# Keeping the attention's output in DRAM as its two float32r parts in a two-layer encoder trunk

## The chip, the cores and the metric

The kernel runs on one core of a Trainium2 chip. The metric is the device time of one execution in microseconds (us). TensorE (PE) multiplies, VectorE (DVE), ScalarE (ACT) and GpSimd (POOL) work on elements, and SyncE (SP) issues all of the DMAs that this text speaks of. SP takes its instructions one after the other, so a DMA that has to wait holds up all that stand behind it.

## The reference, cut to what matters

Two layers over 1024 tokens of 1024 features, in float32. Layer 0 mixes tokens by a neighbourhood attention (NA, 16 heads of 64), layer 1 by a differential attention (DA, 8 heads of 128). Both end in an output projection of the heads' results, which a normalised residual follows:

```python
def neighborhood_attention(h, w_qkv, rpb, w_o):
...
    o = lax.map(row_fn, jnp.arange(rows))
    o = o.transpose(1, 0, 3, 2, 4).reshape(B, S, D)
    return o @ w_o

def diff_attention(h, w_qkv, lam, subln_g, w_o, t5_table, lambda_init):
...
    o = o.transpose(1, 2, 0, 3, 4).reshape(B, DA_HEADS, S, 2 * DA_HEAD_DIM)
    o = rms_norm(o, subln_g) * (1.0 - lambda_init)
    o = o.transpose(0, 2, 1, 3).reshape(B, S, D)
    return o @ w_o
...
        x = x + rms_norm(m, g[1])
        f = conv_glu_ffn(rms_norm(x, g[2]), ffn_w_in[i], ffn_conv_w[i], ffn_conv_b[i], ffn_w_out[i])
```

After that comes a gated feed-forward part of width 2816, and a gate on a per-layer input embedding.

## The kernel before

**The arithmetic.** A float32 matrix is split into two float32r parts: hi, which ACT makes by a copy that rounds, and lo = value - hi, which DVE makes by a subtraction (`split`, L81 to L91; with a scale, lines 88 and 89). A product is then three matmuls: hi by hi, hi by lo, lo by hi.

**The attention's output `oT`** is a scratch tensor in DRAM with the shape (8, 128, 1024): eight head pages (a pair of NA heads, or one DA head) of 128 features by 1024 tokens.
- In NA (`na_values`) the two heads of a pair are added into the page `opage` (tag "oT", one buffer) half by half: ACT copies one half of a PSUM bank to `low` (L434), DVE adds (L435). After the last of a pair's eight chunks L439 stores the page, 512 KB. In the chunk's other work ACT makes the softmax's exponentials (L368), and copies half of the next values' projection to SBUF (L307), which PE then transposes (L135); PE transposes the softmax pages at L410, and ACT and DVE split what comes out. A pair is j, 0 to 7.
- In DA (`da_values`, `da_out`) each of a head's eight chunks of 128 queries ends with its values times the softmax weights (L553), an RMS norm (L556, L557, L119, L559), a transpose on PE (L567), a scaled copy on ACT from PSUM into `ot` (L575, 128x128) and a store of 64 KB (L576). Two `ot` buffers take turns.
- The last page (j or h = 7) is not stored: it stays in SBUF in a buffer of the pool `raw`.

**The output projection.** `out_part(layer, t)` loads the first seven pages of 128 tokens, 448 KB in rows of 512 bytes, into a buffer of `raw` (L646), and splits it into two buffers of `ws`: one ACT instruction and one DVE instruction of 128x896. `raw` has 3 buffers and `ws` has 4, for all of the kernel's loads and split operands. The projection weights `W` come through `raw` too, eight loads of 512 KB (L96) that are split into resident pages.
- `first_out` runs beside the last attention head. It loads and splits W, and does token tile 0 for the first seven pages. `embeddings` runs beside it: it makes eight pages `e` in `ws`, and stores each in `pp` (L1119).
- `mix_out` takes the token tiles in the order 0, 4, 1, 5, 2, 3, 6, 7. For each it multiplies (48 matmuls, L637), normalises and adds the residual. The part of the tile two places later is made ready behind it (`load`, L679 to L683): `out_part`, the split of the last page's 128 columns, and the load of the residual's rows. Two parts fill the four `ws` buffers.

**What sets the order.** PE's order is written out by hand. The other engines' order is set by a scheduler when the kernel is built, from the program's order and what each instruction needs; an instruction stands in its engine's queue and holds up what stands behind it.

Of the kernel before, what the change touches and what calls it, by code (L numbers as in the profile page):

```python
# [8 lines left out]
F32 = mybir.dt.float32  # L9
F32R = mybir.dt.float32r  # L10
AF = mybir.ActivationFunctionType
# [4 lines left out]
P = 128  # L16
D = 1024
SEQ = 1024
NT = SEQ // P
KT = D // P  # L20
# [18 lines left out]
class Trunk:  # L39
# [374 lines left out]
    def na_values(self, x, n, oT):  # L414
        nc = self.nc
        j, m, g = n // 8, n // 4 % 2, n % 4
        V = self.v[2 * j]
        _, _, blocks, hi, lo = self.chunk.pop(n)
        if g % 2 == 0:
            self.o = self.av.tile([P, 512], F32, tag="av", name=self.uid("av"))  # L420
        o = self.o
        steps = [(2 * g, 0, 2, 0), (2 * g + 1, 0, 2, 2)] + [(kb, u, 1, 4 + i) for i, (kb, u) in enumerate(blocks[4:])]
        for i, (kb, u, w, at) in enumerate(steps):
            out = o[:, (2 * g % 4 + u) * P : (2 * g % 4 + u + w) * P]
            for z, a in enumerate((hi, lo)):
                nc.tensor.matmul(  # L426
                    out, V[:, kb, m], a[:, at * P : (at + w) * P], start=i + z == 0, stop=i == len(steps) - 1 and z == 1
                )
        if n % 8 == 0:
            self.opage = self.page(self.raw, "raw") if j == KT - 1 else self.page(x, "oT", bufs=1)  # L430
        if g % 2:
            h = g // 2 * 512
            low = self.page(x, "low", (P, 512), bufs=1)
            nc.scalar.activation(low[0:64], o[64:128], AF.Copy)  # L434
            nc.vector.tensor_tensor(  # L435
                out=self.opage[64 * m : 64 * m + 64, h : h + 512], in0=o[0:64], in1=low[0:64], op=ALU.add
            )
        if n % 8 == 7 and j < KT - 1:
            nc.sync.dma_start(oT[j], self.opage)  # L439

    def na(self, hT, oT, first, mid):

# [119 lines left out]
    def da_out(self, x, n, oT):  # L562
        nc = self.nc
        h, t = n // NT, n % NT
        b, os = self.chunk.pop(n)
        tr = b[:, P : 2 * P]
        nc.tensor.transpose(tr, os, self.ident)  # L567
        cols = slice(t * P, t * P + P)
        if h == D_HEADS - 1:
            if t == 0:  # L570
                self.opage = self.page(self.raw, "raw")
            nc.scalar.activation(self.opage[:, cols], tr, AF.Copy, scale=self.subg)
        else:
            ot = self.page(x, "ot", (P, P))
            nc.scalar.activation(ot, tr, AF.Copy, scale=self.subg)  # L575
            nc.sync.dma_start(oT[h][:, cols], ot)  # L576

    def da(self, hT, oT, first, mid):

# [62 lines left out]

    def out_part(self, layer, t):

        raw = self.page(self.raw, "raw", (P, KT - 1, P))
        self.nc.sync.dma_start(raw, self.oT[layer][: KT - 1, :, t * P : t * P + P].rearrange("j p t -> p j t"))  # L646
        hi, lo = self.page(self.ws, "ws", (P, KT, P), F32R), self.page(self.ws, "ws", (P, KT, P), F32R)
        self.split(raw, hi[:, : KT - 1], lo[:, : KT - 1])
        return hi, lo

    def first_out(self, layer):

# [498 lines left out]

    def run(self):
        i = self.i
        self.oT = [self.scratch(f"oT{n}", (KT, P, SEQ)) for n in range(2)]
        x1 = [self.scratch(f"x1_{n}", (SEQ, D)) for n in range(2)]
        self.pp = [self.scratch(f"pp{n}", (SEQ, D)) for n in range(2)]
        x3 = [self.scratch("x3", (SEQ, D)), self.out]
# [86 lines left out]
```

## Time and profile before

| | us |
|---|---|
| median of 3 runs (lowest to highest) | 2787.24 (2779.03 to 2789.44) |
| the profiled execution, its own time | 2781.16 |
| its span from the first to the last instruction | 2779.2 |
| PE busy | 2703.0 (97%) |
| DVE busy | 1985.5 (71%) |
| ACT busy | 1344.3 (48%) |
| DMA, 298.48 MB | 107 GB/s over the span |

The difference of 2.0 us between the profiled execution's time and its span lies outside of the instructions. Busy time is the sum of an engine's instructions; a stretch in which PE is busy throughout can only grow or shrink with PE's own work, and one in which PE is idle has an idle time that another engine or a transfer ends. The work on `oT` lies in these stretches of the span: NA and its first projections up to about 430 us, the last NA pair with `first_out` up to 490, `mix_out` up to 598; DA from about 1355 to 1890, `first_out` up to 1944, `mix_out` up to 2051.

### The profile page before, as it was taken

The numbers are of one execution on the slowest core, as the hardware profiler recorded it, in microseconds if no ns is written. First come the engines' busy times: TensorE is split into PE (matmuls) and PEld (weight loads), VectorE is DVE, ScalarE is ACT, GpSimd is POOL, SyncE is SP. The second block draws the span as 40 slices with busy tenths as digits, with TensorE's granted clock in tenths as the row PEclk, the third lists the DMA queues.
The fourth block names the chain that finished last, engine by engine and source line by source line (L and its number), as shares of the span: only waits on it lengthen the run. The fifth ranks groups of instructions, "written<-read, shape, count | busy, mean of one in ns | idle before, by whom it ended". The sixth has DMA issues, their size and how long they took to land.

```text
span 2779.2 us, 36486 instructions
## 1 busy us (share of the span) xinstructions
PE 2703.0 (97%) x13312; PEld 2257.8 (81%) x13312; DVE 1985.5 (71%) x3409; ACT 1344.3 (48%) x2491; POOL 498.3 (18%) x473
## 2 busy tenths in 40 slices
PE   7999999989999999999999999999989999999999
PEld 5788888867888888888888888887868888888887
DVE  5677776687777777666677777776687767777664
ACT  4555556443444435454455555566354444444452
POOL 2121220023334300001000000000033343300000
PEclk9999999999999999999999999999999999999999
DMA  6412214623222373343211111115413333272342
GB/s 183 169 52 67 64 49 158 166 71 106 106 96 104 108 266 117 106 143 115 98 45 45 45 46 45 38 38 179 138 64 114 103 103 114 94 285 93 116 149 98
DMA packets 129477, 298.48 MB, mean 107 GB/s; under 512 B 11753, under 2 KB 37737, under 8 KB 129297
## 3 DMA queue, kind: packets, MB, share of 16 engines
q1 hardware_dynamic: 129296, 296.15, 32.4%
q8 instruction: 104, 1.70, 0.3%
q14 instruction: 77, 0.62, 0.1%
HBM read 221.69 MB, written 86.61 MB: 111 GB/s over the span
## 4 chain that ended last, share of the span: by engine, by line
PE 87%; DMA 5%; DVE 4%; ACT 2%; issue 1%; POOL 0%; SPq 0%; ACTq 0%; DVEq 0%; POOLq 0%
PE b L107 20%; PE b L108 20%; PE b L109 20%; PE g L637 5%; PE m L637 5%; PE b L553 4%; PE s L515 2%; PE s L516 2%; PE b L539 2%; PE av L426 2%; PE b L135 2%; PE b L410 1%; DVE r L86 1%; DMA raw<-in_qkv 1%; DMA raw<-in_ple_w_gate 1%
## 5 line engine op out<-in xcount | busy, mean ns | idle before, releaser
L107 PE MATMUL b<-r,ws 128*128 128x512 f32 (+1 forms) x1328 | 549.3, 414 | 12.8 <-ACT r L85 9.5
L109 PE MATMUL b<-r,ws 128*128 128x512 f32 (+1 forms) x1328 | 521.0, 392 | 0.5 <-DVE ws L86 0.5
L108 PE MATMUL b<-r,ws 128*128 128x512 f32 (+1 forms) x1328 | 519.9, 391 | 1.0 <-DVE r L86 0.8
L107 PEld LDWEIGHTS b<-r,ws 128*128 128x128 f32 x1328 | 253.7, 191 | 59.4 <-ACT r L85 11.0
L109 PEld LDWEIGHTS b<-r,ws 128*128 128x128 f32 x1328 | 252.3, 190 | 54.0 <-DVE ws L86 1.0
L119 POOL TENSOR_TENSOR ss<-ss,mhalf 128x1 f32<-128x1 f32 x136 | 90.8, 669 | 1137.4 <-DVE ss L557 566.5
L368 ACT ACTIVATE E<-E,mn 128x1024 f32<-128x1024 f32 (+2 forms) x256 | 221.9, 867 | 147.5 <-DVE mn L364 145.1
L108 PEld LDWEIGHTS b<-r,ws 128*128 128x128 f32 x1328 | 254.2, 191 | 39.7 <-DVE r L86 3.3
L107 PE MATMUL b<-r,wa 128*128 128x512 f32 x688 | 268.6, 390 | 7.5 <-DVE v L906 7.5
L107 PE MATMUL b<-r,r 128*128 128x512 f32 x680 | 268.9, 395 | 4.0 <-DVE v L911 2.9
L108 PE MATMUL b<-r,wa 128*128 128x512 f32 x688 | 268.4, 390 | 0.0
L109 PE MATMUL b<-r,wa 128*128 128x512 f32 x688 | 268.3, 390 | 0.0
L109 PE MATMUL b<-r,r 128*128 128x512 f32 x680 | 265.2, 390 | 0.0
L108 PE MATMUL b<-r,r 128*128 128x512 f32 x680 | 265.2, 390 | 0.0
L86 DVE TENSOR_TENSOR r<-raw,r 128x512 fp32r<-128x512 f32 (+1 forms) x178 | 140.5, 795 | 110.9 <-ACT r L85 110.6
L85 ACT ACTIVATE r<-raw 128x512 fp32r<-128x512 f32 (+1 forms) x178 | 121.4, 689 | 198.7 <-PE b L108 161.6
L86 DVE TENSOR_TENSOR ws<-raw,ws 128x512 fp32r<-128x512 f32 (+3 forms) x168 | 157.6, 946 | 63.2 <-ACT ws L85 61.2
L85 ACT ACTIVATE ws<-raw 128x512 fp32r<-128x512 f32 (+3 forms) x168 | 124.6, 749 | 140.1 <-PE b L109 57.7
L364 DVE CUSTOM_DVE_ANT_0 E<-s,T 128x1024 f32<-128x1024 f32 x128 | 156.5, 1223 | 33.8 <-PE s L516 32.5
L107 PEld LDWEIGHTS b<-r,wa 128*128 128x128 f32 x688 | 129.7, 189 | 35.3 <-ACT cv L916 5.3
L637 PE MATMUL m<-r,ws 128*128 128x512 f32 x672 | 156.7, 392 | 0.0
L637 PE MATMUL g<-r,ws 128*128 128x512 f32 x672 | 155.9, 391 | 0.0
(182 smaller groups left out, 5336.4 us busy)
## 6 DMA issues: line engine op xcount, KB each, us to landing
raw<-in_w_in SPq DMA_DIRECT2D x86, 512.0 KB, 3.5
raw<-in_qkv SPq DMA_DIRECT2D x48, 512.0 KB, 5.6
spillS<-r SPq DMA_DIRECT2D x88, 256.0 KB, 2.7
r<-in_ffn_w_out SPq DMA_DIRECT2D x40, 512.0 KB, 10.1
raw<-spillS SPq DMA_DIRECT2D x40, 512.0 KB, 3.5
spillA<-cv SPq DMA_DIRECT2D x66, 256.0 KB, 2.6
raw<-spillA SPq DMA_DIRECT2D x30, 512.0 KB, 3.7
x<-x SPq DMA_DIRECT2D x24, 512.0 KB, 3.7
```

Source lines behind the costliest of these rows:

```text
L85: nc.scalar.activation(hi, src, AF.Copy)
L86: nc.vector.tensor_tensor(out=lo, in0=src, in1=hi.bitcast(F32), op=ALU.subtract)
L107: mm(out, sta[0], mov[0], start=first, stop=False, skip_group_check=onto)
L108: mm(out, sta[0], mov[1], start=False, stop=False, skip_group_check=onto)
L109: mm(out, sta[1], mov[0], start=False, stop=last, skip_group_check=onto)
L119: self.nc.gpsimd.tensor_tensor(out=ss, in0=ss, in1=self.mhalf, op=ALU.pow)
L135: self.nc.tensor.transpose(t[:, k * P : k * P + P], h[:, c : c + P], self.ident)
L364: nc.vector.tensor_tensor_reduce(out=e, in0=s, in1=bias, scale=1.0, scalar=3e38, op0=ALU.add, op1=ALU.min, accum_out=mn)
L368: nc.scalar.activation(e, e, AF.Exp, bias=mn, scale=-1.0, accum_out=sm)
L426: nc.tensor.matmul(out, V[:, kb, m], a[:, at * P : (at + w) * P], start=i + z == 0, stop=i == len(steps) - 1 and z == 1)
L553: nc.tensor.matmul(o, wT[:, k], V[:, k], start=k == 0, stop=k == KT - 1)
L637: mm(out[half], a, b[:, w], start=first and k + z == 0, stop=last and k == n - 1 and z == 2)
```

## The change

`oT` becomes (2, 8, 128, 1024): hi and lo.
- In NA the finished page is split where it is: ACT writes hi into a new page `oh` (one buffer), DVE writes lo over the page, and two stores of 512 KB take the place of one.
- In DA `ot` holds both parts (128, 2, 128) in one buffer in place of two. ACT's scaled copy writes hi, a new DVE instruction with the scale writes lo from the PSUM bank, and the store has 128 KB.
- `out_part` loads both parts straight into two `ws` buffers, 448 KB each, without `raw` and without a split. The last page of 128 columns is still split in `load`.

```diff
         if n % 8 == 7 and j < KT - 1:
-            nc.sync.dma_start(oT[j], self.opage)
+            hi = self.page(x, "oh", bufs=1)
+            self.split(self.opage, hi.bitcast(F32R), self.opage.bitcast(F32R))
+            for z, a in enumerate((hi, self.opage)):
+                nc.sync.dma_start(oT[z, j], a)
...
         else:
-            ot = self.page(x, "ot", (P, P))
-            nc.scalar.activation(ot, tr, AF.Copy, scale=self.subg)
-            nc.sync.dma_start(oT[h][:, cols], ot)
+            ot = self.page(x, "ot", (P, 2, P), bufs=1)
+            self.split(tr, ot[:, 0].bitcast(F32R), ot[:, 1].bitcast(F32R), self.subg)
+            nc.sync.dma_start(oT[:, h, :, cols].rearrange("z p t -> p z t"), ot)
...
     def out_part(self, layer, t):
 
-        raw = self.page(self.raw, "raw", (P, KT - 1, P))
-        self.nc.sync.dma_start(raw, self.oT[layer][: KT - 1, :, t * P : t * P + P].rearrange("j p t -> p j t"))
-        hi, lo = self.page(self.ws, "ws", (P, KT, P), F32R), self.page(self.ws, "ws", (P, KT, P), F32R)
-        self.split(raw, hi[:, : KT - 1], lo[:, : KT - 1])
-        return hi, lo
+        parts = [self.page(self.ws, "ws", (P, KT, P), F32R) for _ in range(2)]
+        for z, a in enumerate(parts):
+            src = self.oT[layer][z, : KT - 1, :, t * P : t * P + P].rearrange("j p t -> p j t")
+            self.nc.sync.dma_start(a[:, : KT - 1].bitcast(F32), src)
+        return parts
...
-        self.oT = [self.scratch(f"oT{n}", (KT, P, SEQ)) for n in range(2)]
+        self.oT = [self.scratch(f"oT{n}", (2, KT, P, SEQ)) for n in range(2)]
```

From L439 on the changed kernel's lines stand up to three numbers later. PE's and POOL's orders stay as they were; SP, DVE and ACT change at three places above all.

SP at the start of `first_out` of layer 0, before: the last three stores of `e` pages (pp0), the loads of W that stand between them, and the first part of the projection (raw_1053) ahead of four of these.

```order
L1119 DMA pp0_87<-ws_1006_4834 128x1024
L646 DMA raw_1053_5027<-oT0_83 128x7x128
L1119 DMA pp0_87<-ws_1018_4884 128x1024
L96 DMA raw_1056_5033<-in_na_w_o 128x1024
L1119 DMA pp0_87<-ws_1025_4916 128x1024
L96 DMA raw_1057_5037<-in_na_w_o 128x1024
L1119 DMA pp0_87<-ws_1039_4969 128x1024
L96 DMA raw_1058_5041<-in_na_w_o 128x1024
L646 DMA raw_1081_5147<-oT0_83 128x7x128
```

The same place now (ws_1060 and ws_1061 are the first part's hi and lo, ws_1087 and ws_1088 the second's; they take the buffers of the last four `e` pages, in that order):

```order
L1122 DMA pp0_87<-ws_1013_4862 128x1024
L96 DMA raw_1062_5059<-in_na_w_o 128x1024
L1122 DMA pp0_87<-ws_1025_4912 128x1024
L96 DMA raw_1063_5063<-in_na_w_o 128x1024
L96 DMA raw_1064_5067<-in_na_w_o 128x1024
L1122 DMA pp0_87<-ws_1032_4944 128x1024
L651 DMA ws_1060_5055<-oT0_83 128x7x128
L651 DMA ws_1061_5056<-oT0_83 128x7x128
L790 DMA raw_1151_5740<-in_w_in 128x1024
L651 DMA ws_1087_5173<-oT0_83 128x7x128
L1122 DMA pp0_87<-ws_1046_4997 128x1024
```

The first part moves behind the store of the seventh `e` page and all of W's loads, and each of its two loads waits for the store of the `e` page whose buffer it takes.

DVE in DA, at the first chunk of a head, before (E0 is the softmax weights' page that PE transposes next at L539; L250, L255 and L256 belong to the next head's projection):

```order
L544 COPY wT_1941_12379<-b1_1948_12404 128x512
L256 CAST r2_1915_12268<-r2_1915_12268 64x512
L250 TENSOR_TENSOR r2_1915_12268<-b1_1916_12269,r2_1914_12267 64x512
L255 CAST r2_1914_12267<-r2_1914_12267 64x512
L525 RECIPROCAL c_1947_12399<-sum_1946_12397 128x1
L256 CAST r2_1915_12268<-r2_1915_12268 64x512
L526 SCALAR_TENSOR_TENSOR c_1947_12399<-sum_1940_12377,c_1947_12399,neglam_543 128x1
L527 RECIPROCAL sum_1940_12377<-sum_1940_12377 128x1
L528 SCALAR_TENSOR_TENSOR E0_1938_12374<-E1_1944_12394,c_1947_12399,E0_1938_12374 128x1024
```

And now:

```order
L547 COPY wT_1940_12399<-b1_1947_12424 128x512
L256 CAST r2_1914_12287<-r2_1914_12287 64x512
L250 TENSOR_TENSOR r2_1914_12287<-b1_1915_12288,r2_1913_12286 64x512
L255 CAST r2_1913_12286<-r2_1913_12286 64x512
L89 SCALAR_TENSOR_TENSOR ot_1949_12446<-b1_1933_12374,subg_291,ot_1949_12446 128x128
L528 RECIPROCAL c_1946_12419<-sum_1945_12417 128x1
L256 CAST r2_1914_12287<-r2_1914_12287 64x512
L529 SCALAR_TENSOR_TENSOR c_1946_12419<-sum_1939_12397,c_1946_12419,neglam_543 128x1
L530 RECIPROCAL sum_1939_12397<-sum_1939_12397 128x1
L531 SCALAR_TENSOR_TENSOR E0_1937_12394<-E1_1943_12414,c_1946_12419,E0_1937_12394 128x1024
```

The subtraction for the chunk before stands ahead of the instruction that finishes E0; in the other chunks it stands there or right behind it.

DVE in `first_out` of layer 1, before (raw_2945 is W's last block, raw_2942 the first part of the projection, os_2916 what PE's transpose L567 waits for):

```order
L528 SCALAR_TENSOR_TENSOR E0_2899_16636<-E1_2907_16660,c_2910_16665,E0_2899_16636 128x1024
L86 TENSOR_TENSOR r1_2934_16765<-raw_2945_16800,r1_2932_16763 128x1024
L86 TENSOR_TENSOR ws_2944_16797<-raw_2942_16794,ws_2943_16796 128x896
L86 TENSOR_TENSOR ws_2944_16797<-raw_2854_16439,ws_2943_16796 128x128
L364 ISA E0_2919_16719,mn_2920_16720<-s_2918_16714,T_2799_16215 128x1024
```

And now:

```order
L86 TENSOR_TENSOR r1_2933_16833<-raw_2943_16866,r1_2931_16831 128x1024
L528 RECIPROCAL c_2909_16733<-sum_2908_16731 128x1
L529 SCALAR_TENSOR_TENSOR c_2909_16733<-sum_2900_16707,c_2909_16733,neglam_543 128x1
L530 RECIPROCAL sum_2900_16707<-sum_2900_16707 128x1
L531 SCALAR_TENSOR_TENSOR E0_2898_16704<-E1_2906_16728,c_2909_16733,E0_2898_16704 128x1024
L86 TENSOR_TENSOR ws_2942_16863<-raw_2853_16507,ws_2941_16862 128x128
L560 TENSOR_SCALAR ss_2916_16777<-ss_2916_16777 128x1
```

Between E0 and the next softmax two long subtractions are gone: the one of 128x896 altogether, W's to a place ahead of the reciprocals.

In `mix_out` SP's queue holds, per token tile, the two loads of the part two places later in place of one, ahead of the tile's own store; each of them waits for PE's last matmul of the tile whose `ws` buffers it takes.

## Rows read from the trace of the kernel before

**Rows 1.** The page: the shares of the span, by engine, of the chain of work that ended last.

```profile
PE 87%; DMA 5%; DVE 4%; ACT 2%; issue 1%; POOL 0%; SPq 0%; ACTq 0%; DVEq 0%; POOLq 0%
```

**Rows 2.** Busy time by stretch: the stretch in us and its length, then busy us of PE, PEld, DVE, ACT and POOL, PE's granted clock (1.00 is full), the DMA engines' busy share and GB/s. In order: a piece of NA, the last NA pair with the start of `first_out`, the rest of that with `mix_out` of layer 0, its tail, a piece of DA, `first_out` of layer 1, the tail of its `mix_out`.

```profile
100.00:430.00 330.00, 330.00 (x1842) 282.93 (x1841) 244.54 (x631) 185.22 (x434) 69.75 (x91) 1.00 0.19 58
430.00:478.00 48.00, 44.89 (x242) 37.58 (x241) 35.89 (x83) 37.19 (x75) 0.00 (x0) 0.96 0.56 187
478.00:562.00 84.00, 82.68 (x396) 68.84 (x394) 52.01 (x79) 34.30 (x72) 6.60 (x12) 1.00 0.62 170
562.00:598.00 36.00, 25.70 (x121) 20.89 (x118) 32.88 (x53) 19.90 (x41) 5.83 (x4) 0.89 0.28 86
1400.00:1882.00 482.00, 480.92 (x2808) 410.84 (x2807) 366.12 (x719) 270.03 (x537) 30.69 (x54) 1.00 0.13 45
1882.00:1944.00 62.00, 57.82 (x330) 48.02 (x329) 41.83 (x79) 39.29 (x76) 3.85 (x7) 0.98 0.57 191
2015.00:2051.00 36.00, 25.32 (x117) 20.51 (x115) 32.71 (x53) 19.55 (x40) 5.83 (x4) 0.86 0.24 78
```

**Rows 3.** Groups of instructions by line, engine, operation and shape, all over the kernel: count, then busy us and mean ns of one, then idle time of the engine before them and what ended it.

```profile
L86 DVE TENSOR_TENSOR ws<-raw,ws 128x1024 fp32r<-128x1024 f32 x48 | 59.4, 1238 | 31.4 <-ACT ws L85 29.6 <-PE b L491 1.8
L86 DVE TENSOR_TENSOR ws<-raw,ws 128x896 fp32r<-128x896 f32 x16 | 17.4, 1089 | 11.7 <-ACT ws L85 11.7
L86 DVE TENSOR_TENSOR Alo<-b,Ahi 128x128 fp32r<-128x128 f32 x32 | 8.9, 278 | 0.0
L559 DVE TENSOR_SCALAR os<-b,sum,ss 128x128 f32<-128x128 f32 x64 | 26.1, 408 | 1.9 <-POOL ss L119 1.5
```

**Rows 4.** NA, the end of a pair near 181 us, by engine in order of time: start, duration, engine, line; in brackets the engine's idle time before it and what ended that. DVE's subtraction of a transposed softmax piece; ACT's chain behind the addition that completes the page; PE's transposes of what ACT's L307 copies, and its next transposes of this chunk's softmax page.

```profile
184.38 0.69 DVE L86 TENSOR_TENSOR Alo<-b,Ahi 128x512 fp32r<-128x512 f32 x1
...
182.15 0.62 ACT L368 ACTIVATE E<-E,mn 128x384 f32<-128x384 f32 x1 [0.30 <-DVE mn L364]
183.74 0.60 ACT L85 ACTIVATE Ahi<-b 128x512 fp32r<-128x512 f32 x1 [0.28 <-PE b L410]
184.24 1.05 ACT L85 ACTIVATE ws<-raw 128x1024 fp32r<-128x1024 f32 x1
185.19 0.59 ACT L307 ACTIVATE raw<-b 128x512 f32<-128x512 f32 x1
...
185.83 0.65 PE L135 MATMUL b<-ident,raw 128*128 128x128 f32 x4
189.68 0.60 PE L410 MATMUL b<-ident,E 128*128 128x128 f32 x4
```

**Rows 5.** The end of the last stored NA pair: PE's wait there, what stood ahead of L307 on ACT, and the stretch of 2 us behind it, columns as in rows 2.

```profile
440.29 1.12 PE L135 MATMUL b<-ident,raw 128*128 128x128 f32 x4 [1.80 <-ACT raw L307]
...
438.09 1.06 ACT L85 ACTIVATE r<-raw 128x1024 fp32r<-128x1024 f32 x1 [0.15 <-DMA raw<-in_pT]
...
440.00:442.00 2.00, 1.71 (x6) 1.58 (x7) 1.24 (x4) 1.40 (x3) 0.00 (x0) 0.55 0.06 25
```

**Rows 6.** DA: DVE's L255 and E0's last instruction (L528) in a head's first chunk near 1457 us, and PE's transposes of that page; then the same pair in the chunk before.

```profile
1456.29 0.42 DVE L255 CAST r<-r 64x512 fp32r<-64x512 f32 x1
1457.73 1.27 DVE L528 SCALAR_TENSOR_TENSOR E<-E,c,E 128x1024 f32<-128x1024 f32 x1
...
1459.14 0.63 PE L539 MATMUL b<-ident,E 128*128 128x128 f32 x4
...
1446.21 1.27 DVE L528 SCALAR_TENSOR_TENSOR E<-E,c,E 128x1024 f32<-128x1024 f32 x1
...
1450.12 0.60 PE L539 MATMUL b<-ident,E 128*128 128x128 f32 x4
```

**Rows 7.** `first_out` of layer 0: SP's last two issues of `e` stores ahead of the part's first matmul (start, duration, line), then PE's first two matmuls of the output projection (L637).

```profile
469.66 0.33 SPq L1119 DMA_DIRECT2D pp<-ws  x1
472.69 0.32 SPq L1119 DMA_DIRECT2D pp<-ws  x1
...
475.88 0.40 PE L637 MATMUL b<-r,ws 128*128 128x512 f32 x1
477.50 0.50 PE L637 MATMUL b<-r,ws 128*128 128x512 f32 x1 [1.23 <-ACT ws L1118]
```

**Rows 8.** Time from the issue to the landing, least, median and most, of the 16 loads of a part (L646), then of the 16 stores of `e` pages (L1119).

```profile
DMA to landing us min/median/max: 3.6/3.8/5.8
...
DMA to landing us min/median/max: 2.6/3.1/5.3
```

**Rows 9.** `first_out` of layer 1: DVE's two long subtractions, and PE's wait for DVE's L559.

```profile
1914.10 1.22 DVE L86 TENSOR_TENSOR r<-raw,r 128x1024 fp32r<-128x1024 f32 x1
1915.36 1.29 DVE L86 TENSOR_TENSOR ws<-raw,ws 128x896 fp32r<-128x896 f32 x2
...
1919.98 0.33 PE L567 MATMUL b<-ident,os 128*128 128x128 f32 x1 [1.16 <-DVE os L559]
```

**Rows 10.** `mix_out` of layer 0, a token tile: PE's 48 matmuls and the eight transposes behind them, and SP's load of a residual and of a part.

```profile
503.73 11.16 PE L637 MATMUL m<-r,ws 128*128 128x512 f32 x48
514.73 1.03 PE L135 MATMUL b<-ident,h 128*128 128x128 f32 x8
...
503.36 0.55 SPq L682 DMA_DIRECT2D x<-in_x  x1
504.01 0.54 SPq L646 DMA_DIRECT2D raw<-oT  x1
```

## The prediction

> **What bounds the kernel now.** I read first the shares of the chain that ended last: PE holds 87% of it [rows 1], so an edit is worth what it does to PE's idle time and to PE's own work. The change touches no matmul. Next comes the busy time by stretch, where a reader should look at the first figure behind the length: what PE lacks to the full stretch is all that the change can win there. In the stretches that it touches PE lacks 0 us in NA, 48.00 - 44.89 = 3.11 around the last NA pair, 84.00 - 82.68 = 1.32 in `mix_out`, 482.00 - 480.92 = 1.08 in DA, and 62.00 - 57.82 = 4.18 in `first_out` of layer 1, 9.7 us together [rows 2]. The two tails of `mix_out` lack 10.30 and 10.68 us, but there DVE is busy for 32.88 and 32.71 of 36 us [rows 2] with the combining of finished tiles, none of it work on `oT`. So the gain is at most 9.7 us, and the question is which of the new instructions and transfers land on a place where PE has no slack.
>
> **What is moved, in bulk.** DVE loses 16 subtractions of 128x896 at 1.09 us, 17.4 us, and gains seven of 128x1024 at 1.24 us, 8.7, and 56 of 128x128. No row shows that last one, from PSUM with a scale. The nearest are a subtraction from PSUM of the same size, 0.28 us, and L559, from PSUM with two scalars, 0.41 [rows 3]; I take 0.33, nearer to the first, since a subtraction is what it does: 18.5 us. DVE's work grows by some 10 us, and ACT's shrinks. DVE is busy for three quarters of both attention stretches, so the bulk decides nothing; the places do. Every place is taken in turn.
>
> **NA, six pairs (j = 0 to 5): +1.2 us.** ACT's copy of the page, 1.05 us as for W's blocks of that size, stands ahead of the two exponentials at 182.15. From there ACT's chain runs through the split Ahi and the split of a weight block to L307, which ends at 185.19 + 0.59 = 185.78; PE's L135, which needs it, starts at 185.83 [rows 4]. This slack of 0.05 us is the tight place. Ahead of it ACT is idle for 0.30 and for 0.28 us [rows 4], and it gets the page early enough to begin in that gap's place, also saving a little between instructions. Of 1.05 us some 0.85 can be taken by the idle times, by the earlier start and by the overlap that the rows show (1.05 long, next start 0.95 later), so L307 ends some 0.25 later and PE waits for 0.2. Six times 0.2 is 1.2 us. If none were absorbed it would be 6 x 1.05 = 6.3; if all, 0. DVE's subtraction of 1.24 us stands ahead of the reciprocals and delays Alo from 184.38 by that much at most, to an end at 186.3, and by less, since Alo now stands ahead of one scaling of the page; PE's same L135 waits for it as well, which leaves 0.5 at worst, within the 6.3. The softmax page itself is wanted at 189.68 [rows 4], far off. The two stores on SP wait for ACT and for DVE; behind them stand weight loads with a head's time to spare.
>
> **The seventh pair: +0.5.** PE waits here already, for 1.80 us, for L307; ahead of that on ACT stands a split that waits for a load (in_pT) [rows 5]. ACT's copy goes into idle time. The added 512 KB may hold up that load or its followers: 0 to 3.1 us, the median landing of a store of that size [rows 8], and I take 0.5, since the transfers overlap. [...]
>
> **DA: +1.4.** The subtraction stands ahead of E0's last instruction or just behind it. In a head's first chunk DVE runs without a gap from L255 (1456.29) to E0's end, 1457.73 + 1.27 = 1459.00, and PE's transposes of that page begin at 1459.14: 0.14 us of slack [rows 6]. There 0.28 to 0.41 us push PE by 0.14 to 0.27; 0.2 in seven heads is 1.4 us. In the chunk before, E0 ends at 1447.48 and PE comes at 1450.12 [rows 6], 2.6 us of slack that covers the subtraction; without that cover 56 x 0.41 = 23 us. ACT's wait for the one `ot` buffer's store costs nothing: the store before is a chunk old, and the two E0 of [rows 6] stand 11.5 us apart.
>
> [...]
>
> **`first_out` of layer 0: +1.5.** The first part's loads now stand behind the store of the seventh `e` page, issued at 472.69 [rows 7], so hi is issued at 473.0 and lands 3.6 to 5.8 later [rows 8], at 476.6 to 478.8. lo's buffer is free when the store issued at 469.66 [rows 7] has landed, 2.6 to 5.3 later [rows 8], by 475.0 at the latest, and lo lands at 477.0 to 480.8. PE comes for hi at 475.88 and for lo some 0.9 us later; before, its second matmul waited until 477.50 for a copy on ACT [rows 7], which now comes earlier, since a long split ahead of it is gone. [...] Between -0.5 and +5 I take +1.5, from a landing in the middle.
>
> **`first_out` of layer 1: -1.1.** Here the part's subtractions (1.29 us) and the one of W's last block (1.22) stand ahead of L559, for which PE waits 1.16 us at 1919.98 [rows 9]. The first is gone but for its 128 columns, and the second moves ahead, where DVE waits for ACT. The part's loads stand behind W's last block and ahead of the seventh `e` page's store, and no row of before shows when they land; if it is after 1920, the gain is gone. The bounds are +1.5, a late landing as in layer 0, and -1.2.
>
> **`mix_out`: 0.** PE has no gap that the removed splits would close. The doubled loads are covered by the matmuls of one tile, as the first rival tells.
>
> **Sum.** 1.2 + 0.5 + 1.4 + 1.5 - 1.1 = +3.5 us. The profiled execution took 2781.16 us (span 2779.2), which gives 2784.7. It lies 6.1 us under the median of the runs; the same sum on that gives 2787.24 + 3.5 = **2790.7 us**, 0.13% more. About 0.5%, 14 us, is what a measurement of this kernel can tell from no change.
>
> **Rivals.**
> - *Slower: the parts' loads come late in `mix_out`.* Six tiles in each layer, 12, wait with both loads for the matmuls of the tile that frees the buffers. PE then has the transposes of 1.03 us and 48 matmuls of 11.16 [rows 10] before it needs them, 12.2 us. Of these the residual's load that stands ahead on SP takes 0.55 and its own wait, and the two issues 1.1 [rows 10], which leaves 10.5 or less. Against it: both landings overlap, and 3.8 us is the median, 5.8 the worst [rows 8], 7.6 if two medians add up. For it: two of the worst in a row are 11.6, beyond 10.5. [...] I give this 8%.
> - *Slower: DVE's subtraction decides in every chunk of DA.* 23 us in place of 1.4: 2787.24 + 2.1 + 23 = 2812. It would need a slack under 0.41 us everywhere, and [rows 6] show 2.6 in an ordinary chunk. 6%.
> - *Faster: the projection's waits go away and the new ones are hidden.* All 9.7 us of idle time gone would be 2777.5, still within 0.5%; the likely part of it is the 1.1 us above. More would need one of the tails to shrink, by DVE or DMA time freed ahead of it. 4%.
> - That the change does less than it says can be left out: the loads, splits and stores stand in the new order as told.
>
> **How the numbers follow.** The forecast, within 0.5% of before, gets 82%: 2776 to 2801 by its own bounds. The bounds of the terms, DA's 23 us apart (a rival), add up to -1.7 and +17.8 (6.3 + 3.1 + 1.9 + 5 + 1.5), and the runs of before spread over 10 us. The range goes from 2777, where all idle time is gone, to 2806, where the two largest terms, NA and layer 0's `first_out`, are at their upper ends (8.6 us more) and the runs spread upwards by some 6; what lies above belongs to the two slower rivals. Faster 0.04, same 0.82, slower 0.14.
>
> **What would show it.** Right: PE's waits for L307 in six NA pairs at 0.1 to 0.4 us, for E0 in the first chunk of seven heads at 0.1 to 0.3, a wait of 1 to 3 us for a load of `ws` at the first matmul of layer 0's projection, none for L567 near 1920, and no PE wait for `ws` in `mix_out`. Wrong: a wait for `ws` at the start of a tile's 48 matmuls, NA waits near 1 us, or a granted clock under 1.00 where it was 1.00.

## The result, and the profile after

| | before | after |
|---|---|---|
| median of 20 runs (us) | 2784.65 | 2792.09 |
| lowest to highest | 2779.03 to 2789.44 | 2788.12 to 2797.97 |
| the profiled execution, its own time | 2781.16 | 2789.13 |
| its span | 2779.2 | 2787.3 |

The ratio is 1.0029, with a 95% interval of 1.0023 to 1.0035: slower by 7.4 us between the medians, within the 0.5% that count as no change here. The prediction gave 2790.7 us and +3.5. The time came out nearer than the change, which is luck: the prediction started from the 2787.24 us of three runs, and the median of twenty lies 2.6 us lower. Of all the runs compared in this text one, of the kernel half below, took 6439.07 us, and is left out.

The page of the kernel after, its busy times and the shares of the chain, which answer to [rows 1]:

```profile
PE 2706.5 (97%) x13312; PEld 2257.7 (81%) x13312; DVE 1988.6 (71%) x3456; ACT 1334.3 (48%) x2482; POOL 499.4 (18%) x473
...
PE 82%; DVE 7%; DMA 6%; ACT 2%; issue 2%; POOL 0%; SPq 0%; ACTq 0%; DVEq 0%; POOLq 0%
```

DVE, which the change gives more work, is busy for 3.1 us more in all (the prediction had some 10), and ACT for 10.0 less. The sums of work explain nothing, as forecast; the chain names who stands in PE's way more often, DVE and DMA. PE's waits show where. From its tables of waits in three stretches of the kernel after (NA, which has none; the last NA pair with `first_out` and `mix_out` of layer 0, two lines of several; DA, all lines): engine and line, what it waited for, then us in total, times, and the longest.

```profile
PE b L640 <- DMA ws<-oT: 4.2, 1, 4.2
PE b L135 <- ACT raw L307: 1.5, 1, 1.5
...
PE b L542 <- DVE ss L560: 4.0, 14, 0.4
PE b L135 <- ACT wT L545: 0.7, 1, 0.7
PE b L556 <- DVE ot L89: 0.4, 1, 0.4
PE b L542 <- DVE E L531: 0.3, 1, 0.3
```

New are L640's wait of 4.2 us for a part's load, where before stood 1.23 for a copy [rows 7], and in DA 14 waits of L542 with 4.0 us together, where before the table of DA's waits has only the lines for wT and E, 1.0 us in all. 14 is twice the seven heads whose pages are stored.

**Where the time went, by stretch.** PE's 13,312 matmuls stand in the same order in all of the kernels below. So the start of a matmul in one trace less its start in the trace of before is the time lost until then, and the growth of this difference between two matmuls is what a stretch cost. The table gives that growth in us, from one profiled run of each kernel; the stretches are named by the times of before.

| kernel | NA 125 to 428 | `first_out` 0, 428 to 490 | start of `mix_out` 0, 490 to 506 | DA 1355 to 1862 | `first_out` 1, 1862 to 1950 | sum of the five | up to the last matmul |
|---|---|---|---|---|---|---|---|
| after | +0.65 | +4.31 | -1.51 | +5.22 | -1.26 | +7.4 | +8.1 |
| na_only | +0.68 | +4.49 | -1.53 | +0.06 | +0.29 | +4.0 | +7.9 |
| da_only | -0.10 | +0.35 | +0.42 | +5.02 | -2.08 | +3.6 | +1.4 |
| da_nosub | +0.65 | +7.50 | -1.55 | +0.14 | -0.68 | +6.1 | +7.1 |
| da_bank | +0.65 | +6.85 | -1.55 | +1.65 | -0.91 | +6.7 | +5.7 |
| da_pool | +0.67 | +7.08 | -1.55 | +1.40 | -1.10 | +6.5 | +8.9 |
| half | +0.07 | +8.03 | -1.52 | +5.08 | -1.47 | +10.2 | +10.4 |
| early | +0.10 | -1.55 | -1.34 | +5.12 | -0.44 | +1.9 | +6.7 |
| early_pool | +0.07 | -0.19 | -1.55 | +1.52 | -2.32 | -2.5 | -5.2 |
| early_pool, again | +0.03 | -1.63 | -1.53 | +1.64 | -0.94 | -2.4 | -2.4 |
| early_bank | +0.03 | -1.11 | -1.53 | +1.57 | -2.63 | -3.7 | -4.5 |

The five stretches of the kernel after sum to +7.4 us, as much as the medians differ. That they agree so well is partly luck: each row is one profiled run, that of before lies 3.5 us under its median, and the stretches left out (the difference between the last two columns) scatter by some us in kernels that have the same code there. NA, the start of `mix_out` and DA repeat within 0.3 us between kernels with the same code there; `first_out` does not. In the ten other rows the sum of the five lies above the difference of the medians, by 0.7 to 5.2 us. So the table says where, and the medians what it is worth.

**DA, twice per head.** DVE and PE of the kernel after in two chunks of one head, the first and the second: start, duration, engine, line; in brackets PE's idle time and what ended it by the profile. The lines now are L531 for E0 (L528 before), L542 for its transposes (L539), L89 for the new subtraction.

```profile
1459.12 0.35 DVE L89 SCALAR_TENSOR_TENSOR ot<-b,subg,ot 128x128 fp32r<-128x128 f32 x1
...
1460.36 1.27 DVE L531 SCALAR_TENSOR_TENSOR E<-E,c,E 128x1024 f32<-128x1024 f32 x1
...
1467.12 1.26 DVE L531 SCALAR_TENSOR_TENSOR E<-E,c,E 128x1024 f32<-128x1024 f32 x1
1468.30 1.22 DVE L86 TENSOR_TENSOR ws<-raw,ws 128x1024 fp32r<-128x1024 f32 x1
1469.43 0.68 DVE L250 TENSOR_TENSOR r<-b,r 64x512 fp32r<-64x512 f32 x1
1470.14 0.42 DVE L255 CAST r<-r 64x512 fp32r<-64x512 f32 x1
1470.59 0.35 DVE L89 SCALAR_TENSOR_TENSOR ot<-b,subg,ot 128x128 fp32r<-128x128 f32 x1
1470.86 0.14 DVE L560 TENSOR_SCALAR ss<-ss 128x1 f32<-128x1 f32 x1
...
1461.68 0.66 PE L542 MATMUL b<-ident,E 128*128 128x128 f32 x4 [0.23 <-DVE ss L560]
...
1470.04 0.39 PE L518 MATMUL s<-r 128*128 128x512 f32 x1
1470.27 0.39 PE L519 MATMUL s<-r,r 128*128 128x512 f32 x1
1471.00 0.66 PE L542 MATMUL b<-ident,E 128*128 128x128 f32 x4 [0.34 <-DVE ss L560]
```

In the first chunk E0 ends at 1460.36 + 1.27 = 1461.63 and PE starts 0.05 later: the place that the prediction named. In the second chunk E0 has been done since 1468.38, yet PE starts at 1471.00, right after L89's end at 1470.59 + 0.35 = 1470.94. The section on the change has the subtraction ahead of E0's last instruction or right behind it; in each head's second chunk it is neither, since L86, L250 and L255 stand between. The profile writes "ss L560" for both, the nearest event on DVE. It cannot be that instruction: in the same chunk of before PE, DVE and ACT read

```profile
1467.93 0.60 PE L539 MATMUL b<-ident,E 128*128 128x128 f32 x4
...
1468.05 0.15 DVE L557 TENSOR_SCALAR ss<-ss 128x1 f32<-128x1 f32 x1
...
1465.34 0.35 ACT L575 ACTIVATE ot<-b,subg 128x128 f32<-128x128 f32 x1
```

with PE's transposes under way before L557 (now L560) begins. What L542 can need of L89 is a PSUM bank: the transposes take their bank in turn from the two that also hold the chunk's output, and L89 reads that output's bank. Before, its one reader at the end was ACT's L575, which was done at 1465.34 + 0.35 = 1465.69, 2.2 us ahead of PE. One line of the table of waits names L89 outright: L556 (0.4 us) multiplies by wT and reads nothing that L89 writes, so a bank is all that it can wait for. The price is more than the 0.34 us that the row shows: successive matmuls in these rows start 0.23 us apart, so L542 would have started at 1470.50, and PE lost 0.50.

**`first_out` of layer 0.** The timeline of SP of the kernel after (start, duration, line), then ACT's copy that completes the seventh `e` page, and PE at the projection's first matmul:

```profile
468.05 0.33 SPq L1122 DMA_DIRECT2D pp<-ws  x1
468.55 3.66 SPq L96 DMA_DIRECT2D raw<-in_na_w_o  x2
472.26 0.42 SPq L1122 DMA_DIRECT2D pp<-ws  x1
472.79 2.11 SPq L651 DMA_DIRECT2D ws<-oT  x2
...
471.58 0.58 ACT L1121 ACTIVATE ws<-b 128x512 f32<-128x512 f32 x1
...
479.27 1.19 PE L640 MATMUL b<-r,ws 128*128 128x512 f32 x2 [4.24 <-DMA ws<-oT]
```

The time from issue to landing of the store of the sixth `e` page, the one issued at 468.05:

```profile
DMA to landing us min/median/max: 2.9/2.9/2.9
```

Three stretches of 2 us at that matmul, columns as in [rows 2]:

```profile
478.00:480.00 2.00, 0.73 (x2) 0.67 (x3) 0.80 (x2) 0.16 (x1) 0.00 (x0) 0.81 1.13 324
480.00:482.00 2.00, 2.00 (x9) 1.61 (x8) 0.01 (x1) 0.60 (x1) 0.00 (x0) 0.50 1.10 342
482.00:484.00 2.00, 2.00 (x9) 1.58 (x8) 0.97 (x2) 0.28 (x1) 0.00 (x0) 0.83 1.05 406
```

The two loads are issued from 472.79 on, and PE waits until 479.27. The section on the change has each of them wait for a store that frees its buffer; here neither did, since the sixth page's store landed at 468.05 + 2.9, some 471.0, and the fifth's was issued 3.9 us before that one. What held them was their turn on SP: the issue of W's last block ahead of them ends at 468.55 + 3.66 = 472.21, and the seventh page's store comes next, right after ACT has completed that page at 471.58 + 0.58 = 472.16. PE's wait is 4.24 - 1.23 = 3.0 us longer than the one of before [rows 7]. Then the granted clock stands at 0.50 for 2 us and at 0.83 for 2 more: 1.0 + 0.3 = 1.3 us. Together 4.3, near the table's +4.31; the seventh NA pair, which lies in the same stretch, comes out even by 446 us.

**The gains.** In `first_out` of layer 1 the wait of [rows 9] is gone; its table of waits has one for L570 (L567 before) instead of two. The other gain was in no forecast. It stands in layer 0 at the first transposes of `mix_out`. Before, in the timeline of PE, DVE and SP (L752 adds the residual x, and L127, which PE waits for, follows from that):

```profile
502.89 1.09 PE L135 MATMUL b<-ident,h 128*128 128x128 f32 x8 [1.32 <-DVE h L127]
...
498.28 1.23 DVE L752 TENSOR_TENSOR x<-h,x 128x1024 f32<-128x1024 f32 x1 [2.88 <-DMA x<-in_x]
...
482.42 6.14 SPq L646 DMA_DIRECT2D raw<-oT  x3
488.61 1.03 SPq L140 DMA_DIRECT2D g<-in_norm_g  x2
489.69 1.23 SPq L682 DMA_DIRECT2D x<-in_x  x2
```

and after:

```profile
504.99 1.03 PE L135 MATMUL b<-ident,h 128*128 128x128 f32 x8
...
497.85 1.23 DVE L755 TENSOR_TENSOR x<-h,x 128x1024 f32<-128x1024 f32 x1
...
484.76 0.37 SPq L651 DMA_DIRECT2D ws<-oT  x1
485.18 1.52 SPq L140 DMA_DIRECT2D g<-in_norm_g  x2
486.76 1.23 SPq L685 DMA_DIRECT2D x<-in_x  x2
```

Three part loads stood ahead of the residual's load on SP, and SP was done with them at 488.6. Now that load is issued at 486.76, 2.9 us earlier, while PE is 2 to 4 us later there; DVE no longer waits for x, nor PE for DVE.

### The profile page after: what moved, and what is told of

Same layout as the page of the kernel before. It is cut to its first block, busy times and chain, and to the rows that moved or that the text cites. A ratio compares the mean times of both kernels' runs of the same rounds, so it can differ in the third digit from the quotient of the medians.

```text
span 2787.3 us, 36579 instructions
## 1 busy us (share of the span) xinstructions
PE 2706.5 (97%) x13312; PEld 2257.7 (81%) x13312; DVE 1988.6 (71%) x3456; ACT 1334.3 (48%) x2482; POOL 499.4 (18%) x473
## 4 chain that ended last, share of the span: by engine, by line
PE 82%; DVE 7%; DMA 6%; ACT 2%; issue 2%; POOL 0%; SPq 0%; ACTq 0%; DVEq 0%; POOLq 0%
PE b L107 19%; PE b L108 19%; PE b L109 19%; PE g L640 5%; PE m L640 5%; PE b L556 3%; PE b L542 2%; PE s L518 2%; PE s L519 2%; PE b L135 2%; PE av L426 2%; PE b L410 1%; DVE r L86 1%; DMA raw<-in_qkv 1%; DMA r<-in_ffn_w_out 1%
## 5 line engine op out<-in xcount | busy, mean ns | idle before, releaser
L86 DVE TENSOR_TENSOR r<-raw,r 128x512 fp32r<-128x512 f32 (+1 forms) x178 | 140.5, 794 | 109.4 <-ACT r L85 109.0
L86 DVE TENSOR_TENSOR ws<-raw,ws 128x512 fp32r<-128x512 f32 (+2 forms) x152 | 141.5, 932 | 77.2 <-ACT ws L85 49.6
L85 ACT ACTIVATE ws<-raw 128x512 fp32r<-128x512 f32 (+2 forms) x152 | 110.7, 728 | 149.5 <-PE b L109 57.7
L640 PE MATMUL m<-r,ws 128*128 128x512 f32 x672 | 155.9, 391 | 0.0
L640 PE MATMUL g<-r,ws 128*128 128x512 f32 x672 | 155.9, 391 | 0.0
```

What stands on the lines that cost most here:

```text
L85: nc.scalar.activation(hi, src, AF.Copy)
L86: nc.vector.tensor_tensor(out=lo, in0=src, in1=hi.bitcast(F32), op=ALU.subtract)
L640: mm(out[half], a, b[:, w], start=first and k + z == 0, stop=last and k == n - 1 and z == 2)
```

## The experiments

**The theories.** For DA: (1) PE waits for the PSUM bank, which DVE's subtraction frees later than ACT's copy did; the rival (2) is that the subtraction's time on DVE delays E0, in two chunks instead of one. For `first_out` of layer 0: (3) the loads come late because of the `e` pages, whose `ws` buffers they take and behind whose stores they stand; the rival (4) is that what NA adds, its copies and its two stores, makes the stretch late. Each kernel is the changed one with the edit that is shown, and each ratio stands against runs of the kernel before on the same chip.

**na_only and da_only: one layer at a time.** In na_only DA's end and `out_part` of layer 1 are those of before, in da_only the page's store in NA and `out_part` of layer 0 (the new `out_part` stands under the last line of each cut, the old one behind it):

```diff
-            ot = self.page(x, "ot", (P, 2, P), bufs=1)
-            self.split(tr, ot[:, 0].bitcast(F32R), ot[:, 1].bitcast(F32R), self.subg)
-            nc.sync.dma_start(oT[:, h, :, cols].rearrange("z p t -> p z t"), ot)
+            ot = self.page(x, "ot", (P, P))
+            nc.scalar.activation(ot, tr, AF.Copy, scale=self.subg)
+            nc.sync.dma_start(oT[h][:, cols], ot)
...
+        if layer == 0:
```

> The change in layer 0 alone; layer 1 keeps its page in one float32 part and its split in the projection. If the late loads of the first part in layer 0 (+4.6 us at the projection's first matmul, -1.5 given back in the output loop) and ACT's copy in the six pairs (+0.6) are the cause, it is +3 to +4.5 us over before, with one PE wait for a ws load of about 4 us and no new wait in the differential attention. If layer 0's cost was chance of the profiled execution, it is within 1 us of before.

Measured: 2786.11 us, 1.0004 (0.9995 to 1.0013), less than was expected. `first_out` of layer 0 shows its wait of 4.4 us, DA none of its 14.

```diff
-            hi = self.page(x, "oh", bufs=1)
-            self.split(self.opage, hi.bitcast(F32R), self.opage.bitcast(F32R))
-            for z, a in enumerate((hi, self.opage)):
-                nc.sync.dma_start(oT[z, j], a)
+            nc.sync.dma_start(oT[j], self.opage)
...
+        if layer == 1:
```

> The change in layer 1 alone. If the subtraction in the differential attention costs 0.75 to 0.8 us per head (7 heads, +5.8) and the projection gives 1.8 us back, it is +4 us over before. If the 2.7 us that the trace loses near 2060 and 2085 us by a lower granted clock are also the change's, it is +6 to +7. If the differential attention cost only the 0.2 us per head that the prediction told, it is within 1 us of before.

Measured: 2786.94 us, 1.0007 (0.9998 to 1.0015), again less than was expected. DA's 14 waits are there, 3.9 us, and the stretch costs +5.02. So by the traces each loss comes with its own layer's part. By the medians the halves are worth 1.4 and 2.2 us, together 3.6 beside the whole's 7.4; with intervals of some 2.5 us each that is near the edge of what fits, and the traces, which give +4.0 and +3.6, add up better.

**da_nosub: the subtraction alone taken away.** The values are those of hi alone, stored twice; lo is left out in DA.

```diff
-            ot = self.page(x, "ot", (P, 2, P), bufs=1)
-            self.split(tr, ot[:, 0].bitcast(F32R), ot[:, 1].bitcast(F32R), self.subg)
-            nc.sync.dma_start(oT[:, h, :, cols].rearrange("z p t -> p z t"), ot)
+            ot = self.page(x, "ot", (P, P))
+            nc.scalar.activation(ot.bitcast(F32R), tr, AF.Copy, scale=self.subg)
+            for z in range(2):
+                nc.sync.dma_start(oT[z, h][:, cols], ot)
```

> The whole change without the subtraction in the differential attention: hi is stored twice, 64 KB each, and the lo part of layer 1's stored pages holds hi, so the subtraction is left out. If the subtraction is the cost, by the bank or by DVE's time, all of 5.8 us goes: +1.5 to +2.5 over before. If the doubled store is the cost (the buffer's wait, or the transfer), it stays at +7.

Measured: 2785.64 us, 0.9997 (0.9989 to 1.0006), 0.9 us over before and under what was expected; DA +0.14. The stores, as large as the change's, cost nothing; all of DA's loss hangs on the subtraction. (The edit also gives `ot` its two buffers back; da_bank, next, keeps the one.)

**da_bank: the subtraction kept on DVE, the bank given back by ACT.** ACT copies the scaled tile to SBUF; both parts are made from that.

```diff
-            ot = self.page(x, "ot", (P, 2, P), bufs=1)
-            self.split(tr, ot[:, 0].bitcast(F32R), ot[:, 1].bitcast(F32R), self.subg)
+            ot, full = self.page(x, "ot", (P, 2, P), bufs=1), self.page(x, "of", (P, P), bufs=1)
+            nc.scalar.activation(full, tr, AF.Copy, scale=self.subg)
+            nc.scalar.activation(ot[:, 0].bitcast(F32R), full, AF.Copy)
+            nc.vector.tensor_tensor(out=ot[:, 1].bitcast(F32R), in0=full, in1=ot[:, 0], op=ALU.subtract)
```

> The whole change, but in the differential attention ACT copies the transposed tile to SBUF in float32, makes hi from that, and DVE subtracts there, so that the PSUM bank is free when ACT has read it. Theory of the bank (PE waits in each head's second chunk because DVE's subtraction reads the bank late): the 0.5 us at each head's second chunk go, 3.5 us of the 7.4, which leaves +4. Rival, DVE's time (its instruction delays the softmax page's last step or the next softmax): nothing changes, +7 to +8.

Measured: 2787.62 us, 1.0011 (1.0002 to 1.002); DA +1.65. PE's wait in DA by the table of waits:

```profile
PE b L542 <- DVE ss L560: 1.9, 7, 0.3
```

the new subtraction's group in that stretch (count, busy us and mean ns of one, idle before), and PE and DVE in the second chunk of the head shown above:

```profile
L580 DVE TENSOR_TENSOR ot<-of,ot 128x128 fp32r<-128x128 f32 x55 | 15.8, 286 | 0.7
...
1473.18 0.60 PE L542 MATMUL b<-ident,E 128*128 128x128 f32 x4
...
1473.26 0.29 DVE L580 TENSOR_TENSOR ot<-of,ot 128x128 fp32r<-128x128 f32 x1
```

Seven of the 14 waits are left, with DVE's instruction still there at 286 ns in place of 345. An instruction that is 59 ns shorter cannot give back 3.6 us at seven places. The rows show it directly: the subtraction still stands late, but PE's transposes now start 0.08 us before it begins, where in the kernel after they started only at its end. Theory (1) holds for the second chunks, 5.22 - 1.65 = 3.6 us, 0.5 each. The rest, 1.65 / 7 = 0.24 each, is the delay of E0, theory (2), in the first chunks alone.

**da_pool: the subtraction from SBUF, on GpSimd.** As da_bank, with one word changed:

```diff
-            nc.vector.tensor_tensor(out=ot[:, 1].bitcast(F32R), in0=full, in1=ot[:, 0], op=ALU.subtract)
+            nc.gpsimd.tensor_tensor(out=ot[:, 1].bitcast(F32R), in0=full, in1=ot[:, 0], op=ALU.subtract)
```

> The whole change, with the float32 copy on ACT as in the run that freed the bank early, and the subtraction on POOL in place of DVE. Theory: both parts of the differential attention's cost go (3.5 us by the bank, 1.65 us by DVE's time in each head's first chunk), under 0.3 us between 1355 and 1862; total +2 to +3 over before. [...]

Measured: 2787.49 us, 1.0014 (1.0005 to 1.0023); DA +1.40, where under 0.3 was expected. The seven waits stay, 1.9 us, though nothing is left on DVE that was not there before. DVE and POOL at the first chunk show why:

```profile
1461.44 0.65 DVE L255 CAST r<-r 64x512 fp32r<-64x512 f32 x1
...
1461.36 0.45 POOL L580 TENSOR_TENSOR ot<-of,ot 128x128 fp32r<-128x128 f32 x1 [5.55 <-issue]
```

POOL's subtraction begins just ahead of DVE's L255, which takes 0.65 us beside it instead of 0.42 [rows 6], and hands on 0.23 us to E0, as much as the subtraction itself had. L255 starts 0.08 us after POOL's instruction and ends 0.28 us after it, at 1462.09 against 1461.81. Over DA the 30 of L255 take 472 ns in the mean, where in da_bank they take 422: 1.5 us in all, about DA's +1.40. Why the cast takes longer beside POOL was not shown.

**early: three of the `e` pages out of `ws`, and NA's split by halves.** In layer 0 every third `e` page takes a buffer of its own, so that the first part's loads need not wait for the last stores; NA splits the page in two halves of 512 columns, each when it is finished.

```diff
-            e = self.page(self.ws, "ws")
+            e = self.page(x, "e", bufs=1) if layer == 0 and t % 3 == 1 else self.page(self.ws, "ws")
...
-        if n % 8 == 7 and j < KT - 1:
+        if n % 4 in (1, 3) and m == 1 and j < KT - 1:
+            hi, w = self.page(x, "oh", (P, 512), bufs=1), slice(h, h + 512)
...
```

> The whole change, with three of layer 0's eight e pages in a buffer of the attention's own pool, so that the first part's two loads find their ws buffers free two pages earlier; the page's split in the neighbourhood attention is done in two halves of 512 columns, which makes the room. Theory (the loads stand behind the store of the seventh e page and wait for the buffers of the fifth and sixth): PE's wait of 4.2 us for the load goes to 1.3 or less, and the total falls by 3 to 4.5, to +3 to +4 over before. Rival (DMA traffic holds the loads up wherever they stand): the wait stays over 3 us and the total at +7.

Measured: 2784.6 us, 1.0001 (0.999 to 1.0011), 0.6 us over before and better than expected. SP and PE at the same place as above:

```profile
469.50 1.21 SPq L651 DMA_DIRECT2D ws<-oT  x2
...
476.43 0.50 PE L640 MATMUL b<-r,ws 128*128 128x512 f32 x1 [0.45 <-ACT e L1121]
```

The loads go out 3.3 us earlier, now right behind the store of the sixth `e` page and ahead of W's last two blocks, and PE waits 0.45 us for a copy instead of 4.24 for a load. From issue to landing the transfers into and out of `ws` between 470 and 500 us take 6.8 us in the median there, against 6.1 in the kernel after; it is the issue that moved. The edit frees buffers and with that changes the order on SP. The two were not tried apart; the trace of the kernel after points to the order. `first_out` costs -1.55, NA +0.10, DA still +5.12.

**half: NA's split by halves alone**, early without the `e` buffer, to tell (3) from (4).

> The whole change, with the neighbourhood attention's page split in two halves of 512 columns when each is complete, and nothing else. Theory: the wait for layer 0's first part stays at 4 us or more and the differential attention's 5 us stay, so the total is at +6 to +8 over before; only the 0.1 us per pair in the neighbourhood attention go. Rival: the halves, not the earlier loads, made the gain of the run with the e pages moved: +3 to +4, with a wait under 1.5 us.

Measured: 2791.34 us, 1.0027 (1.0017 to 1.0038). NA is at +0.07, and `first_out` as bad as ever, with PE's wait for the load at

```profile
PE b L640 <- DMA ws<-oT: 5.7, 1, 5.7
```

half and early both keep NA's copies and stores, and differ in the `e` buffer alone, with the wait in one and not in the other. So NA's part is not what makes the wait: (4) falls, (3) holds. The halves mend NA and are worth no more than its 0.6 us.

**early_pool and early_bank: both mends together.** early with da_pool's edit (run twice) and with da_bank's.

> Both mends together. By the places: first part -1 to 0 against before, output loop of layer 0 -1.5, projection of layer 1 -1 to -2, attentions 0 to +1: 1 to 4 us under before, ratio 0.9985 to 0.9995. If the savings of the output loop were only the shadow of the late start, it is at before's time or 1 us over.

> The version with both mends once more, beside the two others on the same chip: 0.998 to 0.9996 of before, as in its first run. If that run was chance, its interval holds 1.

> Early loads in layer 0, and the PSUM bank freed by ACT with the subtraction on DVE. By the places: attentions +1.5 to +2, first part -1 to 0, output loop -1.5, projection of layer 1 -1: between -2 and 0 against before, ratio 0.999 to 1.000. If the subtraction on POOL was what made the faster version, it is 3 us above that one.

Measured: early_pool 2780.72 us, 0.9988 (0.9979 to 0.9996), and again on another chip 2779.89, 0.9988 (0.9979 to 0.9997); early_bank 2778.8, 0.9987 (0.9978 to 0.9996), faster than expected, and no slower than the two with POOL. All three intervals lie under 1. The change with both mends is worth some 0.12%, 3.5 us. How much of that is the change's is not shown: no run gave the kernel before the `e` buffer alone, and with it PE's wait for a copy at this place is 0.45 us where before has 1.23. Against da_bank (1.0011) and da_pool (1.0014) the freed buffers and NA's halves give back 0.24 to 0.26%, near 7 us. That is much for the one wait of 4.2 us, and fits with what follows it at a lowered clock, 1.3 us in the kernel after.

## Why the prediction was right or wrong

The time lay in the range, slower and within 0.5% as forecast; the sum was half of what came, +3.5 against +7.4. Even that is nearer than its terms, which miss in both directions:

| term | forecast | measured in the stretch |
|---|---|---|
| NA, six pairs and the seventh | +1.2 + 0.5 | +0.65 up to 428; the seventh even (a wait of 1.5 us, not 1.80, then 0.6 and 0.8) |
| DA | +1.4 | +5.2 |
| `first_out` of layer 0 | +1.5 | +4.3 (4.3 to 8.0 over six kernels with this order) |
| `mix_out` | 0 | -1.5 |
| `first_out` of layer 1 | -1.1 | -1.3 (-0.4 to -2.6 over the kernels with this code) |

**NA was right in kind and over-sized.** ACT's rows of the kernel after, at the pair of [rows 4]:

```profile
180.41 1.05 ACT L85 ACTIVATE oh<-oT 128x1024 fp32r<-128x1024 f32 x1
181.36 0.61 ACT L368 ACTIVATE E<-E,mn 128x384 f32<-128x384 f32 x1
...
183.04 1.05 ACT L85 ACTIVATE ws<-raw 128x1024 fp32r<-128x1024 f32 x1
183.99 0.58 ACT L307 ACTIVATE raw<-b 128x512 f32<-128x512 f32 x1
...
184.63 0.66 PE L135 MATMUL b<-ident,raw 128*128 128x128 f32 x4
```

The copy runs without a gap into the exponentials, as told, and L135 starts 0.06 us after L307's end at 184.57, still the tight place. Six pairs cost 0.65 us, 0.1 each instead of 0.2; no wait of it is long enough to be listed. The copy was absorbed for nine tenths, not for four fifths.

**DA is the step that failed**: "In the chunk before, E0 ends at 1447.48 and PE comes at 1450.12 [rows 6], 2.6 us of slack that covers the subtraction". That is true of E0, and the first chunks cost what was forecast (0.24 us each by da_bank, 0.2 by the prediction). But L539 takes two things, its operand and a PSUM bank to write into, and the prediction counted the slack of the operand only. The edit moved the bank's last reader from ACT, which had ended L575 2.2 us before PE came, to DVE, where in each head's second chunk 2.3 us of other work (L86, L250, L255) stand between E0 and it; "ahead of E0's last instruction or just behind it" missed that place. Seven times 0.50 is 3.5 us, nearly all of the 3.8 that this term missed: shown by da_bank, which gives the bank back from ACT and keeps the DVE instruction. The prediction read the change's cost on DVE as a duration; here it is a position in DVE's queue.

The subtraction itself took 345 ns over 56, against 330 taken, between the two rows that bounded it. In the kernel after:

```profile
L89 DVE SCALAR_TENSOR_TENSOR ot<-b,subg,ot 128x128 fp32r<-128x128 f32 x56 | 19.3, 345 | 0.5
```

**`first_out` of layer 0 was right in mechanism, and the landing mis-sized.** The loads stood behind the seventh `e` store and went out at 472.79, as worked out (473.0). PE could start at 479.27, which is past the bound for hi; the bounds had hi at 476.6 to 478.8 and lo at 477.0 to 480.8. Behind the longer wait the clock fell, to 0.50 and then 0.83, which cost 1.3 us that the value of +1.5 does not hold. Against the 477.11 (475.88 + 1.23) at which PE's wait of before ended, these landings alone reach +2.8, 1.7 by hi and 1.1 more by lo, for which PE comes 0.9 us later; the rest of the bound of +5 was the author's estimate, which no run shows, and what the kernel after showed in its place is the 1.3 us. The middle was taken from the landings of before; the 32 loads of parts, most of which go out in pairs, show from issue to landing, least, median and most,

```profile
DMA to landing us min/median/max: 3.7/5.1/7.4
```

against 3.6, 3.8 and 5.8 for the loads of before [rows 8], 11 of 16 of which go out on their own: in the kernel after they landed later, and the upper end was the one to take. Here two blocks of W and a store were issued in the 4.3 us before as well, and no run tells their share. The sign that the prediction set, a wait of 1 to 3 us for a load, came at 4.2, and so did one of its signs of being wrong, a granted clock of 0.50 where it was 1.00.

**`mix_out` lost a wait that the prediction denied.** "PE has no gap that the removed splits would close" holds for the splits. But the 1.32 us that PE lacked there by [rows 2] were one wait, behind a residual that stood behind three part loads on SP, and the change moved these. The prediction worked out the 1.32 and did not ask which wait it was. The traces show this cause, and no run tested it by itself; the gain comes in every kernel with layer 0's part of the change, in early too, where PE is not late, and not in da_only (+0.42). The first rival, loads that come late in `mix_out`, did not come about: PE waits for no load of `ws` in it in either layer, even at the longer landings, up to 7.4 us.

**Layer 1's `first_out`** went as told: the long subtractions no longer stand ahead of os, and its loads were in time.

**Open.** Between 2051 and 2100 the kernel after loses 2.7 us more at a lower granted clock (0.50 and 0.62 over 2056 to 2064 and 0.71 over 2088 to 2092 by its own times, where before has 0.66 over 2052 to 2056 and 1.00 behind it). So do early (+2.8) and da_pool (+2.8), but da_bank (+0.0) and half (+0.2) do not, and all have the same code there; it is put down to scatter between runs, which was not settled. The spread of `first_out` in layer 0 from 4.3 to 8.0 us is open too: PE's wait for the load in these kernels goes from 4.2 to 5.7 us, and what sets its length was not tried.

## What to carry to other kernels

When an edit gives a PSUM bank another last reader, look at what stands ahead of that reader in its engine's queue, and at who writes the bank next. Here a DVE instruction of 345 ns cost PE 0.50 us at seven places by where it stood, and copying the tile out first on the engine that used to free the bank won 3.6 of DA's 5.2 us back. When loads go straight into operand buffers instead of a staging pool, look at who held those buffers, give a holder that is late a buffer of its own, and look where the loads then stand in the queue: here they went out at 472.79, behind the store of the seventh `e` page, and with buffers of their own for three of these pages 3.3 us earlier, with PE's wait at 0.45 us in place of 4.24. A wait's label can name the nearest event on the engine (here L560), so compare it with the same place of the old trace before believing it, and take a PE wait at its shown length plus the start that pipelined matmuls would have had (here 0.34 us shown and 0.50 lost, with starts 0.23 apart).

## What was not expected of the hardware

- Part loads of 448 KB, 28 of 32 of them issued in pairs, landed after 5.1 us in the median, 7.4 at most, where those of before, 11 of 16 issued on their own, took 3.8 and 5.8.
- A subtraction of 128x128 took 286 ns on DVE from SBUF, and on POOL 947 ns in the mean of 56, 0.45 to 1.42 us in the rows from 1425 to 1475; DVE's cast beside it took 0.65 us in place of 0.42. Taking the subtraction off DVE in this way left DA at +1.40, against +1.65 with it on DVE.
- A wait of 4.24 us on PE was followed by 4 us at a lowered granted clock (0.50, then 0.83), and one of 5.7 us, in half, by 4 us at 0.50: 1.3 us and 2.0 us on top of the waits.
